# Row-wise infinity norm: the last 128 rows as a block of their own, transposed on VectorE and stored as one line

## The chip, the core and the metric

The kernel runs on one core of a Trainium2 chip. The metric is the device time of one execution in microseconds (us); the time of a kernel is the median over its runs. Profiles are of one execution each. PE is TensorE, DVE is VectorE, ACT is ScalarE, POOL is GpSimd, SP is SyncE.

## The reference

```python
def setup_inputs():
    return {"x": np.random.randn(8192, 8192).astype(np.float32)}

def reference(x):
    return np.linalg.norm(x, ord=np.inf, axis=1)
```

With a vector per row, this is the largest absolute value of each of the 8192 rows: 256 MiB (268.4 MB) in, 32 KB out.

## The kernel before

The work is one stream. SyncE issues loads of x into a ring in SBUF (`ring`, three places of 16384 columns, 128 partitions), and VectorE reduces each landed load with an absolute maximum (`Pieces.reduce`, line 110 in the profile). `Pieces.load` (line 92) issues the loads. There are five semaphores for loads, `SEMS = 5`, each counting one load at a time: load i is issued once the reduction of load i - 5 is done, and once the reductions that still read its place in the ring are done. The first three loads wait for nothing.

The rows come in two groups. The first 46 x 128 = 5888 rows are the big ones: partition p holds 46 rows that follow each other in memory, and a load brings two of them (`R = 2`, 16384 columns) to each partition, 23 loads in all, reduced by one instruction each into `res_big`. The last 18 x 128 rows are the tail: partition p holds 18 rows that follow each other (`x_tail`), and the loads cut this run of 18 x 8192 columns wherever `tail_loads` puts a cut. `tail_loads` plans the cuts from the end backwards. It has a price for a load (1.1775 ns a column and 0.073 us) and for a reduction (1.0417 ns a column and 0.060 us), and picks each width so that VectorE is done with what came before when the load lands. The planned tail has 29 loads from 16384 columns down to 704, so there are 52 loads in all, 24 of them of 16384 columns.

A load that crosses from one row to the next is reduced by one instruction for each row. A row with several pieces leaves partial results in a tile `parts`, and GpSimd combines them (line 207) into the row's column of `res_tail`. The very last row of each partition is done otherwise: its partial results go to columns of `ring` just behind the place where its last load lands, so that the last reduction takes the 704 landed columns and the 6 partial results in one go, 710 elements, and no combining comes after it.

At the end three stores go out, all of them 128 pieces, one for each partition:

- `early` (line 220, ACT's queue): the 46 columns of `res_big`, 23 KB.
- `middle` (line 224, ACT's queue): the first 16 columns of `res_tail`, 8 KB. It waits for GpSimd's work on these rows.
- `last` (line 239, SyncE's queue): the last two columns of `res_tail`, 1 KB, that is 8 bytes for each partition. It waits for VectorE's last reduction, behind which stand two tiny idle memsets (line 218), and a no-op on line 235 has waited for GpSimd.

`early` and `middle` also wait for the reduction of the third load from the end.

Of the kernel before, what the change touches and what calls it, by code (L numbers as in the profile page):

```python
# [7 lines left out]
P = 128  # L8
R = 2
RING = 3 * 16384  # L10
APART = 2048
SEMS = 5


LOAD = (1.1775e-3, 0.073)
REDUCE = (1.0417e-3, 0.060)
SPARE = 0.08
ROWS = 18
FIRST = 768
SNAP = 0.6  # L20
GRAIN = 64

IDLE = 2


def tail_loads(n_cols, big):

    slack = 0.0
    lag = REDUCE[0] * FIRST + REDUCE[1]
    loads = []
    end = ROWS * n_cols

    def take(top, bottom, most):
        nonlocal slack  # L40
        w = 0
        n = 0
        spare = SPARE if loads else 0
        while True:

            n += 1
            start = max(bottom, (top - 1) // n_cols * n_cols - (n - 1) * n_cols)
            fit = int((lag + slack - spare - REDUCE[1] * n) / REDUCE[0])
            w = max(w, min(fit, top - start) // GRAIN * GRAIN)
            if fit <= top - start or start <= bottom:  # L50
                break
        w = max(GRAIN, min(w, most, top - bottom))
        row = (top - w + n_cols - 1) // n_cols * n_cols
        if top - row >= SNAP * w or (w == most and top > row):
            w = top - row
        n = (top - 1) // n_cols - (top - w) // n_cols + 1
        slack += (LOAD[0] - REDUCE[0]) * w + LOAD[1] - REDUCE[1] * n
        loads.append((top - w, w))
        return top - w

    ends = [take(end, end - n_cols, FIRST), take(end - n_cols, end - 2 * n_cols, n_cols)]
    for top, bottom in zip(ends, (end - n_cols, 0)):
        while top > bottom:
            top = take(top, bottom, big)
    return loads[::-1]


class Pieces:
# [57 lines left out]
@with_exitstack  # L126
def kernel(
    ctx: ExitStack,
    tc: tile.TileContext,
    x: bass.AP,  # L130
    out: bass.AP,
):
    nc = tc.nc
    f32 = mybir.dt.float32
    n_rows, n_cols = x.shape

    tail = tail_loads(n_cols, R * n_cols)
    split = n_rows - ROWS * P
    n_big = split // (R * P)

    x_big = x[:split].rearrange("(p t r) m -> t p (r m)", p=P, r=R)
    x_tail = x[split:].rearrange("(p r) m -> p (r m)", p=P)

    single = ctx.enter_context(tc.tile_pool(name="single", bufs=1))
    ring = single.tile([P, RING + APART], f32)
    res_big = single.tile([P, n_big, R], f32)
    res_tail = single.tile([P, ROWS], f32)
    idle = single.tile([1, IDLE], f32)  # L150
    pieces = Pieces(tc, ring)

    for t in range(n_big):
        at = pieces.room(R * n_cols)
        pieces.load(at, R * n_cols, x_big[t])
        buf = ring[:, at : at + R * n_cols]
        pieces.reduce([(res_big[:, t, :], buf.rearrange("p (r m) -> p r m", r=R))])


    parts = []  # L160
    for i, (start, w) in enumerate(tail):
        c = 0
        while c < w:
            row = (start + c) // n_cols
            n = min(w - c, (row + 1) * n_cols - start - c)
            parts.append((row, i, c, n))
            c += n
    of_row = [[q for q in parts if q[0] == row] for row in range(ROWS)]

    spots, behind, dst = {}, {}, {}
    at = RING
    for row, own in enumerate(of_row):
        if row == ROWS - 1:
            spots[own[-1][1]] = at
            at += own[-1][3]
            for q in own[:-1]:
                dst[q] = ring[:, at : at + 1]
                at += 1  # L180
            behind[own[-1]] = len(own) - 1
            dst[own[-1]] = res_tail[:, row : row + 1]
        elif len(own) == 1:
            dst[own[0]] = res_tail[:, row : row + 1]
        else:
            some = single.tile([P, len(own)], f32, name=f"parts{row}")
            for k, q in enumerate(own):
                dst[q] = some[:, k : k + 1]
    assert at <= RING + APART and len(behind) == 1
    for i, (start, w) in enumerate(tail):  # L190
        at = spots[i] if i in spots else pieces.room(w)
        pieces.load(at, w, x_tail[:, start : start + w])
        done = pieces.reduce(
            [
                (dst[q], ring[:, at + q[2] : at + q[2] + q[3] + behind.get(q, 0)])
                for q in parts
                if q[1] == i
            ]
        )
        for row in range(ROWS - 1):  # L200
            if len(of_row[row]) > 1 and of_row[row][-1][1] == i:
                best = dst[of_row[row][0]]
                more = [dst[q] for q in of_row[row][1:]]
                while more:
                    two, more = more[:2], more[2:]
                    to = best if more else res_tail[:, row : row + 1]
                    combined = nc.gpsimd.tensor_scalar(  # L207
                        out=to,
                        in0=best,
                        scalar1=two[0],  # L210
                        scalar2=two[1] if len(two) == 2 else None,
                        op0=mybir.AluOpType.max,
                        **(dict(op1=mybir.AluOpType.max) if len(two) == 2 else {}),
                    )
                    tc.add_to_no_dep_group("combined", combined.ins)
    tc.declare_fence(done.ins, group="loads")
    for i in range(IDLE):
        tc.keep_in_program_order(nc.vector.memset(idle[:, i : i + 1], 0.0))  # L218

    early = nc.scalar.dma_start(  # L220
        out=out[:split].rearrange("(p q) -> p q", p=P), in_=res_big.rearrange("p t r -> p (t r)")
    )
    out_tail = out[split:].rearrange("(p r) -> p r", p=P)
    middle = nc.scalar.dma_start(
        out=out_tail[:, : ROWS - 2], in_=res_tail[:, : ROWS - 2]
    )
    for store in (early, middle):
        tc.add_manual_dep(
            store.ins,
            pieces.last[-3].name,  # L230
            mybir.DependencyInfo(mybir.DependencyClass.Sync, mybir.DependencyReason.DATA),
            reason="not beside the last load",
        )

    seen = nc.sync.keepalive_nop([nc.sync.lower_ap(res_tail[:, ROWS - 2 : ROWS - 1])])
    tc.keep_in_program_order(seen)
    tc.no_tile_sem_insts.add(seen.ins.name)
    tc.add_to_no_dep_group("seen", seen.ins)
    last = nc.sync.dma_start(out=out_tail[:, ROWS - 2 :], in_=res_tail[:, ROWS - 2 :])
    tc.declare_no_dep(last.ins, group="combined", reason="SyncE has waited for GpSimd")  # L240
    tc.declare_fence(last.ins, group="seen")
# [1 line left out]
_INS = ['x']  # L243
_OUTS = [((8192,), 'float32')]
# [25 lines left out]
```

## Time and profile before

| | |
|---|---|
| median of 3 runs | 629.04 us (628.88 to 629.17) |
| span of the profiled execution, first to last instruction | 627.3 us |
| that execution's own time beside its span | not given apart; the median stands 1.74 us above the span |
| VectorE busy | 552.1 us (88%), 62 instructions |
| GpSimd busy | 3.2 us |
| bytes read from HBM | 268.44 MB, 428 GB/s over the span |

How to read it. The span runs from the first to the last instruction that the profile has; launch and completion lie outside. A group's row gives line, engine, operation, output and input, number, busy time in total, mean duration in nanoseconds, and the idle time of the engine ahead of it with what ended it. A timeline row gives start, duration, engine, line, operation and shape; `SPq` and `ACTq` are the queues of an engine that issues DMAs, and their rows tell of the issue and not of the transfer. A row of the DMA issues gives the number of issues, their size, and the time from issue to landing. Rows of 40 digits cut the stretch asked for into 40 equal slices, each digit being the busy share in tenths.

### The profile page before, as it was taken

The numbers are of one execution on the slowest core, as the hardware profiler recorded it, in microseconds if no ns is written. First come the engines' busy times: TensorE is split into PE (matmuls) and PEld (weight loads), VectorE is DVE, ScalarE is ACT, GpSimd is POOL, SyncE is SP. The second block draws the span as 40 slices with busy tenths as digits, with TensorE's granted clock in tenths as the row PEclk, the third lists the DMA queues.
The fourth block names the chain that finished last, engine by engine and source line by source line (L and its number), as shares of the span: only waits on it lengthen the run. The fifth ranks groups of instructions, "written<-read, shape, count | busy, mean of one in ns | idle before, by whom it ended". The sixth has DMA issues, their size and how long they took to land.

```text
span 627.3 us, 175 instructions
## 1 busy us (share of the span) xinstructions
DVE 552.1 (88%) x62; POOL 3.2 (1%) x14
## 2 busy tenths in 40 slices
DVE  0588988889988889888898888988889999999998
POOL 0000000000000000000000000000000000000000
DMA  9999999999999999999999999999999999999997
GB/s 401 405 464 401 468 401 468 401 468 401 468 401 468 401 468 401 468 401 468 401 460 410 456 414 447 422 443 426 435 424 442 411 430 440 430 424 430 425 423 304
DMA packets 7921, 268.48 MB, mean 428 GB/s; under 512 B 1264, under 2 KB 1264, under 8 KB 2416
## 3 DMA queue, kind: packets, MB, share of 16 engines
q1 hardware_dynamic: 7632, 268.44, 99.3%
q10 hardware_dynamic: 288, 0.03, 0.0%
q14 instruction: 1, 0.01, 0.0%
HBM read 268.44 MB, written 0.03 MB: 428 GB/s over the span
## 4 chain that ended last, share of the span: by engine, by line
DMA 57%; DVE 42%; issue 0%; DVEq 0%; SPq 0%
DMA ring<-in_x_dram 57%; DVE res_big L110 22%; DVE parts L110 12%; DVE res_tail L110 7%; DVE ring L110 1%; DVEq L265 0%; SPq L92 0%; DVE idle L218 0%
## 5 line engine op out<-in xcount | busy, mean ns | idle before, releaser
L110 DVE TENSOR_REDUCE res_big<-ring 128x2 f32<-128x16384 f32 x23 | 396.1, 17220 | 69.6 <-DMA ring<-in_x_dram 69.6
L110 DVE TENSOR_REDUCE parts<-ring 128x1 f32<-128x3136 f32 (+18 forms) x22 | 78.5, 3633 | 1.2 <-DMA ring<-in_x_dram 1.2
L110 DVE TENSOR_REDUCE res_tail<-ring 128x1 f32<-128x8192 f32 (+1 forms) x9 | 69.8, 7811 | 2.1 <-DMA ring<-in_x_dram 2.1
L110 DVE TENSOR_REDUCE ring<-ring 128x1 f32<-128x1600 f32 (+5 forms) x6 | 8.3, 1445 | 0.0
L207 POOL TENSOR_SCALAR res_tail<-parts 128x1 f32<-128x1 f32 x9 | 2.7, 296 | 615.7 <-DVE parts L110 615.7
L207 POOL TENSOR_SCALAR parts<-parts 128x1 f32<-128x1 f32 x1 | 0.4, 353 | 5.6 <-DVE parts L110 5.6
L254 POOL MEMSET const-bfloat16-1.0<- 128x1 bf16 x1 | 0.1, 102 | 0.0
L254 POOL MEMSET const-uint8-127<- 128x1 uint8 x1 | 0.1, 101 | 0.0
L254 POOL MEMSET const-float32-0.0<- 128x1 f32 x1 | 0.1, 98 | 0.2 <-issue 0.2
L254 POOL MEMSET const-float32-1.0<- 128x1 f32 x1 | 0.1, 98 | 0.0
L218 DVE MEMSET idle<- 1x1 f32 x2 | 0.1, 59 | 0.0
## 6 DMA issues: line engine op xcount, KB each, us to landing
ring<-in_x_dram SPq DMA_DIRECT2D x3, 4096.0 KB, 40.5
ring<-in_x_dram SPq DMA_DIRECT2D x1, 7264.0 KB, 31.1
ring<-in_x_dram SPq DMA_DIRECT2D x1, 5024.0 KB, 33.3
ring<-in_x_dram SPq DMA_DIRECT2D x1, 4544.0 KB, 34.5
ring<-in_x_dram SPq DMA_DIRECT2D x1, 4224.0 KB, 40.3
ring<-in_x_dram SPq DMA_DIRECT2D x1, 4032.0 KB, 35.5
ring<-in_x_dram SPq DMA_DIRECT2D x1, 3584.0 KB, 35.4
ring<-in_x_dram SPq DMA_DIRECT2D x2, 1568.0 KB, 18.3
```

Source lines behind the costliest of these rows:

```text
L110: ins = self.nc.vector.tensor_reduce(out=dst, in_=src, axis=mybir.AxisListType.X, op=mybir.AluOpType.max, apply_absolute_value=True,)
L207: combined = nc.gpsimd.tensor_scalar(out=to, in0=best, scalar1=two[0], scalar2=two[1] if len(two) == 2 else None, op0=mybir.AluOpType.max, ...
L218: tc.keep_in_program_order(nc.vector.memset(idle[:, i : i + 1], 0.0))
L254: nc = _bacc.Bacc("TRN2", target_bir_lowering=False, num_devices=1)
```

## The change

The tail is divided. The 17 x 128 rows ahead of the last 128 keep the layout with rows that follow each other in a partition (`x_tail`, now 17 rows a partition). The last 128 rows are a block of their own, one row for each partition (`x_last`). So the results of the last block are 128 numbers that lie beside each other in the output. The last reduction writes them to column 0 of a new tile `res_last` (128 x 32, cleared by a memset at the start of the kernel); four VectorE transposes of 32 x 32 bring that column into one partition of a tile `line` (32 x 128), and SyncE stores this partition's 512 bytes in one piece. The transposes stand between the last reduction and the idle memsets.

`tail_loads` is gone, and a written list `TAIL` has the widths: 29 loads, now from 11392 and 15744 down to 704 and 640, with an 832 among them. With 23 big loads there are again 52. The order at the end is changed: the last 704 columns of row 16, the last of the 17, are loaded next to last, after all but the last 640 columns of the last block. Both of these rows now use the columns of `ring` behind their last load for partial results: row 16 has 4 of them, the last block 7. In the built program the tail has 44 reductions where it had 37, and GpSimd has 13 combining operations where it had 10.

`middle` now stores all 17 columns of `res_tail` in pieces of 68 bytes. Its wait for the third load from the end is gone; it waits for the reduction of row 16, which is the next to last, and for GpSimd. The no-op that waited for GpSimd on SyncE is gone, and SyncE's store waits for the last transpose.

```diff
-tail = tail_loads(n_cols, R * n_cols)
-split = n_rows - ROWS * P
+ROWS = 17
+TAIL = [11392, 15744, 14016, 12480, 11136, 9856, 8832, 7872, 6976, 6208, 5440, 4864, 4352, 3840]
+TAIL += [3456, 3008, 2688, 2432, 2112, 1856, 832, 1536, 1344, 1152, 1024, 896, 768, 704, 640]
...
+    split = n_rows - (ROWS + 1) * P
+    split_last = n_rows - P
...
-    x_tail = x[split:].rearrange("(p r) m -> p (r m)", p=P)
+    x_tail = x[split:split_last].rearrange("(p r) m -> p (r m)", p=P)
+    x_last = x[split_last:]
...
+    res_last = single.tile([P, 32], f32)
+    line = single.tile([32, P], f32)
+    nc.vector.memset(res_last, 0.0)
...
+    last_row = ROWS * n_cols
+    tail = []
+    at = 0
+    for w in TAIL[:-2]:
+        tail.append((at, w))
+        at += w
+        if at + TAIL[-2] == last_row:
+            at = last_row
+    tail += [(last_row - TAIL[-2], TAIL[-2]), (at, TAIL[-1])]
...
-        if row == ROWS - 1:
+        if row >= ROWS - 1:
             spots[own[-1][1]] = at
...
-            dst[own[-1]] = res_tail[:, row : row + 1]
+            dst[own[-1]] = res_last[:, 0:1] if row == ROWS else res_tail[:, row : row + 1]
...
-        pieces.load(at, w, x_tail[:, start : start + w])
+        of_last = start - last_row
+        src = x_tail[:, start : start + w] if of_last < 0 else x_last[:, of_last : of_last + w]
+        pieces.load(at, w, src)
...
     tc.declare_fence(done.ins, group="loads")
+    for q in range(P // 32):
+        own = slice(q * 32, q * 32 + 32)
+        tc.keep_in_program_order(nc.vector.transpose(out=line[:, own], in_=res_last[own, :]))
     for i in range(IDLE):
         tc.keep_in_program_order(nc.vector.memset(idle[:, i : i + 1], 0.0))
...
-    out_tail = out[split:].rearrange("(p r) -> p r", p=P)
     middle = nc.scalar.dma_start(
-        out=out_tail[:, : ROWS - 2], in_=res_tail[:, : ROWS - 2]
+        out=out[split:split_last].rearrange("(p r) -> p r", p=P), in_=res_tail
     )
-    for store in (early, middle):
-        tc.add_manual_dep(
-            store.ins,
...
+    tc.add_manual_dep(
+        early.ins,
...
-    seen = nc.sync.keepalive_nop([nc.sync.lower_ap(res_tail[:, ROWS - 2 : ROWS - 1])])
...
-    last = nc.sync.dma_start(out=out_tail[:, ROWS - 2 :], in_=res_tail[:, ROWS - 2 :])
-    tc.declare_no_dep(last.ins, group="combined", reason="SyncE has waited for GpSimd")
-    tc.declare_fence(last.ins, group="seen")
+    nc.sync.dma_start(out=out[split_last:].rearrange("(o q) -> o q", o=1), in_=line[0:1, :])
```

## The prediction

> **What bounds the kernel now.** I began with the page: which engine is busy, then the slices and the chain.
>
> ```profile
> span 627.3 us, 175 instructions
> DVE 552.1 (88%) x62; POOL 3.2 (1%) x14
> DMA  9999999999999999999999999999999999999997
> ...
> HBM read 268.44 MB, written 0.03 MB: 428 GB/s over the span
> ```
>
> The DMA row is full in 39 slices of 40: the input stream sets the length, and VectorE (DVE), 88% busy, follows it. The chain that ended last gives the pace.
>
> ```profile
> 59.27 40.78 DMA ring<-in_x_dram
> 100.06 0.03 issue
> 100.08 17.23 DVE res_big L110
> ...
> 623.38 0.71 issue
> 624.09 0.89 DVEq L265
> 624.97 0.01 DVE idle L218 x2
> ```
>
> Its pieces start again every 58.05 us, which is three loads of 16384 columns: 19.35 us a load, 1.18 ns a column. VectorE takes 17.23 us for the same columns. It needs 0.89 of a load's time, so a load that follows one of w columns may be as short as some 0.89 w before VectorE falls behind. Small loads cost something beyond their bytes on both sides. The rest is the end of the span, by the timeline and the DMA issues of its last microseconds.
>
> ```profile
> 623.35 0.38 ACTq L220 DMA_DIRECT2D out_dram<-res_big  x1
> 623.77 0.45 ACTq L224 DMA_DIRECT2D out_dram<-res_tail  x1
> 624.09 0.88 DVE L110 TENSOR_REDUCE res_tail<-ring 128x1 f32<-128x710 f32 x1
> 624.35 0.36 POOL L207 TENSOR_SCALAR res_tail<-parts 128x1 f32<-128x1 f32 x1 [10.82 <-DVE parts L110]
> 624.92 0.06 DVE L218 MEMSET idle<- 1x1 f32 x2
> 625.00 0.35 SPq L239 DMA_DIRECT2D out_dram<-res_tail  x1
> ```
>
> ```profile
> ring<-in_x_dram SPq DMA_DIRECT2D x1, 352.0 KB, 4.1
> out_dram<-res_big ACTq DMA_DIRECT2D x1, 23.0 KB, 1.7
> out_dram<-res_tail ACTq DMA_DIRECT2D x1, 8.0 KB, 2.4
> out_dram<-res_tail SPq DMA_DIRECT2D x1, 1.0 KB, 1.5
> ```
>
> The last load (704 columns, 352 KB) was issued at 619.97 and landed 4.1 us later, at 624.07. Its reduction starts at 624.09 and ends at 624.97, the last store is issued at 625.00 and lands 1.47 us later (1.5 in the row) at 626.47, and the span ends at 627.3, 0.8 us behind. So 3.2 us of the span lie behind the stream. The change can move the time in two places only: the 624 us of stream, and these 3.2 us. The median of the runs, 629.04, stands 1.74 us above the span of 627.3; I make the sum on the span and add 1.74.
>
> **The stream.** Bytes and number of loads stay: 24 + 28 = 52 before, 23 + 29 = 52 after, each with one row of each of 128 partitions, so whatever a load costs beyond its bytes is paid 52 times in both. What could lengthen the stream is a queue that runs dry, since a load is issued when the reduction five loads back, and what lay in its part of the ring, are done. I stepped through the new list with the prices of the rows. A reduction of 256 columns takes 409 ns and one of 768 takes 942, so 1.041 ns a column and 142 ns fixed, of which 83 overlap the one before (624.09 lies 0.08 before 623.23 + 0.94): 0.06 us each. A load: the 24th had landed at 467.75, where its reduction starts in the timeline, and the last at 624.07, so 28 loads brought 131072 columns in 156.3 us; with 19.35 us for 16384, that makes 1.176 ns a column and 0.076 us a load. The same stepping puts the last reduction of the kernel before at 624.06, where the timeline has 624.09. With the new list it gives: VectorE idle only once in the tail (3.0 us before the load of 15744); from there every reduction within 0.1 us of its landing, but for the 832 columns, 1.0 us late and caught up at the next load; each of the last loads issued at least 2.8 us before the one ahead of it lands (before: 3.2). The first load took about 1 us from issue to its first bytes, so the queue does not run dry. The tail has 44 reductions instead of 37; 7 x 0.06 = 0.4 us, within VectorE's idle time. The last load lands at 624.05: **0.0**.
>
> New is the address pattern of the last 8192 columns: rows 32 KB apart, where the tail before has 18 rows (576 KB) and the big loads 46 rows (1.5 MB) between partitions. The trace shows the same rate at both of those, as the stepping with a single price fits both. The Trainium skill (DMA: Bandwidth & Descriptors, Latency and other measured facts) speaks against powers of two: 207 instead of 214 GB/s at a pitch of 512 KiB, 103 at 4 MiB. Its nearest case, 3.3% on the last block, would add an estimated 0.3 us; no run here shows such a pitch. By the rows, the last block costs 8192 x 1.18 = 9.7 us, 0.1 us for each per cent that it slows. From above, the slices of the page go down to 401 GB/s where the mean is 428, 6.3% or +0.6 us; from below 0, since no row shows the stream faster than its pace. I take 0, by the two pitches that the trace has.
>
> **Behind the last landing, on the path.** *Last reduction*: 640 columns and 7 partial results instead of 704 and 6, so 647 instead of 710 elements: 63 x 1.041 ns = **-0.06 us**, end at 624.91.
>
> *Four transposes*, 32x32 each, between the reduction and the store. The first waits for the reduction's own completion, 0.02 us by the chain's "issue" pieces. The trace has no transpose. From below: four idle memsets at 59 ns, 0.24 us. From above: four of GpSimd's one-column operations at 296 ns, 1.18 us. The nearest row is VectorE's own reduction: 142 ns fixed + 32 x 1.041 = 175 ns alone, 92 with the overlap, so 175 + 3 x 92 = 0.45 us. A transpose must take in its block before it gives it out, which argues for more; I take **+0.50** and the wait's **+0.02**, and the last transpose ends at 625.43. The memsets now run behind it and SyncE doesn't wait for them (**-0.01**).
>
> The Trainium skill (VectorE: DVE Perf Modes, The TRN2 errata) gives about 150 cycles fixed at 0.96 GHz. That would be an estimated (150 + 32) / 0.96 = 190 ns each with nothing overlapped, 0.76 us for the four; the overlap of 0.08 us in the rows above speaks for less.
>
> *Store*, one line of 512 bytes instead of 128 pieces of 8 bytes. The DMA view of 625.00 to 626.60 shows where the 1.47 us went (a digit is 0.04 us):
>
> ```profile
> DMA  0000000000000000000003543100000000000000
> ...
> q1 hardware_dynamic: 144, 0.00, 4.8%
> ```
>
> Packets run from 625.84 to 626.04: 0.84 us of making descriptors, 0.20 of packets, 0.43 of confirmation. One packet takes away nearly all of the 0.20, and with one share instead of 16 there is no last of 16 to wait for: **-0.22**, landing 1.25 after the issue. From below I allow 1.0 (descriptors made faster too), from above the 2.4 of the 8 KB store.
>
> *Other stores.* `middle` now carries row 16 of the tail and waits for the reduction before the last: 623.23 + 0.88 = 624.11 instead of 623.77. With its 2.4 us it lands at 626.55, 0.15 before the line store; it is the next late one, and would take over if the line landed sooner. ACT has nothing queued behind it. SyncE's wait for GpSimd goes; it ended when the operation of 624.35 was done, 0.27 before VectorE, so nothing comes of it. GpSimd's 3 more operations of 0.3 us and the memset of `res_last`, which runs in the 22.7 us that VectorE waits for its first load, are hidden.
>
> **Sum.** -0.06 + 0.02 + 0.50 - 0.01 - 0.22 = +0.23 us: issue at 625.45, landing at 626.70, span 627.5, time 629.04 + 0.23 = 629.3. Ends of the unknown terms: transposes at 0.24 and a landing in 1.0 give -0.3 us, or 628.7; transposes at 1.18 alone give +0.9, or 629.9, and the slower last block with them +1.5, or 630.5; a landing in 2.4 alone gives +1.4, or 630.4.
>
> **Rivals.** What this kernel's measurement can tell from no change is about 0.2%, 1.26 us.
> 1. *The line store lands late.* It goes through one share of one queue, and whatever delays that share delays the end. For it: the 8 KB store took 2.4 us and the 23 KB store before it 1.7, so size does not decide. Against: the 1 KB store, alone in time, took 1.5. At 2.4 us the sum is +1.4 us, 630.4; with transposes at 0.45 it crosses 1.26 from a landing of 2.35 us. Slower.
> 2. *The stream slows in the tail*, by the new pitch or by loads issued too late. From 13% on the last block (1.26 / 9.7) it crosses the bound; half of that gives 629.9. Against: the full DMA row at two pitches, and 2.8 us of cover. At 13%, 630.5. Slower.
> 3. *The end shrinks.* A store that lands in 1.0 us and transposes at 0.24 give 628.7, but then `middle` holds the end at 626.55, and the time is 629.1. To gain 1.26 of the 3.2 us behind the stream would need the store nearly free. Only a faster stream, which the single price per column does not suggest, gives 627.7.
>
> **How the numbers follow.** The sum above, within 0.2%: 0.64. Rival 1: 0.17, and rival 2: 0.14, of which a part stays within the bound; together they give slower 0.26 and same 0.05. Rival 3: 0.05, nearly all of it faster by a cause I don't see (0.04). So faster 0.04, same 0.70, slower 0.26. The time is that of the sum, 629.3; the range goes from 628.7 (both end terms low) to 630.5 (one rival in full).
>
> **What would show it.** In the changed profile: last reduction starting at 624.1 and ending at 624.9; four transposes within 0.5 us; a store of 0.5 KB with 1.2 to 1.3 us to landing; VectorE waiting for DMA once, some 3 us, in the tail; span 627.5. A last reduction starting later than 624.3 makes the stream's step wrong; transposes over 0.2 us each, or a landing over 1.5, the end's.

## The result and the profile after

The changed kernel takes 630.15 us (630.02 to 630.5, 14 runs) against 628.9 us (628.78 to 629.17, 14 runs) in the same session: a ratio of 1.002, 95% interval 1.0013 to 1.0027. That is 1.25 us more, just at the 0.2% that I had set for "no change", and inside the range. The interval leaves out 1, so the loss is real, if small. The forecast time, 629.3, was 0.85 us too low.

The first lines of the page of the changed kernel, to be held against those of the kernel before:

```profile
span 628.4 us, 191 instructions
DVE 553.5 (88%) x74; POOL 4.0 (1%) x17
DMA  9999999999999999999999999999999999999997
HBM read 268.44 MB, written 0.03 MB: 427 GB/s over the span
```

The span is 1.1 us longer, the DMA row as full as before. Its timeline from 624.5 us on (start, duration, engine, line, operation):

```profile
623.91 0.88 DVE L64 TENSOR_REDUCE res_tail<-ring 128x1 f32<-128x708 f32 x1
624.71 0.82 DVE L64 TENSOR_REDUCE res_last<-ring 128x1 f32<-128x647 f32 x1
624.89 0.34 ACTq L197 DMA_DIRECT2D out_dram<-res_tail  x1
625.56 0.84 DVE L190 STREAM_TRANSPOSE line<-res_last 32x32 f32<-32x32 f32 x4
626.36 0.07 DVE L192 MEMSET idle<- 1x1 f32 x2
626.43 0.32 SPq L206 DMA_DIRECT2D out_dram<-line  x1
```

Three things are to be read off. The last reduction starts at 624.71 and not at 624.09, so 0.62 us were lost ahead of it, in the stream. Four transposes take 0.84 us. And the store is issued at 626.43; SyncE's waits tell when it landed (engine, line, what it waited for: total, times, longest):

```profile
SPq L230 <- DMA out_dram<-line: 0.7, 1, 0.7
```

SyncE's issue ends at 626.75, the next instruction is through at 626.83, and 0.7 us later the store has landed: 627.54, 1.11 us after the issue, where the 8-byte pieces took 1.47.

| from the two traces | before | after | step |
|---|---|---|---|
| last reduction starts | 624.09 | 624.71 | +0.62 |
| last reduction takes | 0.88 | 0.82 | -0.06 |
| from its end to the store's issue | 0.03 | 0.90 | +0.87 |
| from issue to landing | 1.47 | 1.11 | -0.36 |
| span | 627.29 | 628.36 | +1.07 |

The remaining 0.18 us of the 1.25 belong to the one profiled run of the kernel before. In all runs on record with both numbers the time stands 1.73 to 1.83 us above the span, so its span of 627.29 goes with a time of about 629.07, which is 0.17 above the median of 628.9.

Where the 0.62 us come from, the waits show (window from 500 us to the end, the changed kernel first, then the kernel before):

```profile
DVE parts L64 <- DMA ring<-in_x_dram: 0.7, 1, 0.7
```

```profile
DVE parts L110 <- DMA ring<-in_x_dram: 1.2, 1, 1.2
```

The wait of the kernel before ended at 496.8, ahead of a reduction that reaches into the window; from there to the end its VectorE waits for no load. The wait of the changed kernel lies inside the window, and the timeline of VectorE from 570 to 585 us puts it in its place:

```profile
579.26 5.88 DVE L64 TENSOR_REDUCE parts<-ring 128x1 f32<-128x1984 f32 x2 [0.72 <-DMA ring<-in_x_dram]
```

This is the load of 5440 columns, a width with nothing special, well ahead of the last block. It landed 7.34 us behind the one before it, where 5440 x 1.176 ns + 0.076 = 6.47. In the DMA view of 576 to 577 us a second queue appears:

```profile
q1 hardware_dynamic: 21, 0.46, 110.9%
q14 instruction: 1, 0.01, 2.0%
```

The kernel before has it in its last three microseconds and nowhere else in its span (view of 624.3 to 625.3 us):

```profile
q14 instruction: 1, 0.01, 1.9%
```

In the changed kernel it is one packet of 8 KB of instructions, 576.17 to 576.50. The row packets of that load took 0.81 to 0.82 us each on their share of the queue, except one, which started at 576.49 and took 1.47. Each load has 16 completions. Ahead of the packet the last of them follows the one before it by 0.05 us; from this load on by 0.86 to 0.91, and still so three loads from the end. The share that had met the packet did not catch up, and a load counts as landed when its last share is there. In the last two loads the distance falls to 0.40 and 0.10 us, because the other shares come later there; the loads themselves still land at their price, 0.87 and 0.80 us apart where it gives 0.90 and 0.83. This became theory B; its rivals were the widths, the row pitch, and the code of another engine.

### The profile page after: what moved, and what is told of

It reads as the page before. It is cut to its first block, busy times and chain, and to the rows that moved or that the text cites. A ratio compares the mean times of both kernels' runs of the same rounds, so it can differ in the third digit from the quotient of the medians.

```text
span 628.4 us, 191 instructions
## 1 busy us (share of the span) xinstructions
DVE 553.5 (88%) x74; POOL 4.0 (1%) x17
## 4 chain that ended last, share of the span: by engine, by line
DMA 59%; DVE 40%; issue 0%; DVEq 0%
DMA ring<-in_x_dram 59%; DVE res_big L64 22%; DVE parts L64 11%; DVE res_tail L64 4%; DVE ring L64 3%; DVE res_last L64 0%; DVE line L190 0%; DVEq L230 0%; DVE idle L192 0%
## 5 line engine op out<-in xcount | busy, mean ns | idle before, releaser
L64 DVE TENSOR_REDUCE parts<-ring 128x1 f32<-128x3712 f32 (+23 forms) x27 | 104.6, 3938 | 3.6 <-DMA ring<-in_x_dram 3.6
L64 DVE TENSOR_REDUCE res_tail<-ring 128x1 f32<-128x8192 f32 (+1 forms) x5 | 35.6, 7117 | 0.0
L64 DVE TENSOR_REDUCE ring<-ring 128x1 f32<-128x1088 f32 (+10 forms) x11 | 16.4, 1566 | 0.0
```

Source lines behind the costliest of these rows:

```text
L64: ins = self.nc.vector.tensor_reduce(out=dst, in_=src, axis=mybir.AxisListType.X, op=mybir.AluOpType.max, apply_absolute_value=True,)
```

## The experiments

Spans are of one profiled execution, ratios of the medians against the kernel before in the same session. The place of the instruction packet (one packet of 8 KB in the span, in every profile) and the last reduction's start are what tells the theories apart:

| run | VectorE instructions in the program (the profile lists 2 fewer in each) | packet at, us | last reduction starts | span |
|---|---|---|---|---|
| before | 71 | 624.87 | 624.09 | 627.29 |
| changed | 84 | 576.17 | 624.71 | 628.36 |
| e1 no transposes, 128 pieces | 80 | 576.02 | 624.58 | 633.32 |
| e2 changed + 24 on VectorE | 108 | 394.20 | 624.54 | 628.19 |
| e3 before + 24 on VectorE | 95 | 413.74 | 624.75 | 627.90 |
| e4 changed + 24 on GpSimd | 84 | 576.20 | 624.75 | 628.40 |
| e5 changed, one transpose | 81 | 576.23 | 624.78 | 628.30 |
| e6 own block, old cuts, four transposes | 76 | 624.43 | 624.02 | 627.75 |
| e7 the same, one transpose | 73 | 624.48 | 624.07 | 627.66 |
| e8 before, 4-byte pieces | 71 | 624.57 | 624.12 | 627.27 |
| e9 e6 + 8 on VectorE | 84 | 550.60 | 624.67 | 628.39 |
| e10 new widths, shorter code | 76 | 582.71 | 624.83 | 628.36 |
| e11 before + 24 on GpSimd | 71 | 624.55 | 624.05 | 627.20 |
| e12 new widths, shorter still | 74 | 582.58 | 624.68 | 628.20 |

**e1.** The end without the transposes.

```diff
-    for q in range(P // 32):
-        own = slice(q * 32, q * 32 + 32)
-        tc.keep_in_program_order(nc.vector.transpose(out=line[:, own], in_=res_last[own, :]))
...
-    nc.sync.dma_start(out=out[split_last:].rearrange("(o q) -> o q", o=1), in_=line[0:1, :])
+    nc.sync.dma_start(out=out[split_last:].rearrange("(p o) -> p o", o=1), in_=res_last[:, 0:1])
```

> The changed kernel without the four transposes: the 128 results of the last block go out in 128 pieces of 4 bytes, straight from the column that the last reduction writes. Theory A (the end of the span is a chain of a wait, four transposes of 0.20 us one behind the other, and a store): the store is issued 0.87 us sooner after the last reduction and lands in about 1.47 us as the 8-byte pieces of the kernel before did, instead of 1.11; the span shrinks from 628.4 by 0.87 - 0.36 = 0.5 us to 627.9. Rival (the one-line store is not quicker by itself, the store lands in 1.1 us here too): 627.5. In both the last load still lands near 624.6, since nothing of the stream is touched, if the 0.56 us there do not hang on the transposes.

Measured: 635.28 us, ratio 1.0101 (1.0084 to 1.0118), span 633.3. Both expected spans, 627.9 and 627.5, were more than 5 us too low. The issue came as early as expected, 0.03 us after the last reduction (0.90 with the transposes). The landing did not; the row of the issue in the timeline, and the last row of the DMA issues (KB, us to landing):

```profile
625.42 0.35 SPq L203 DMA_DIRECT2D out_dram<-res_last  x1
```

```profile
out_dram<-res_last SPq DMA_DIRECT2D x1, 0.5 KB, 7.1
```

So 128 pieces of 4 bytes side by side in the output land in 7.1 us. With the results of a block beside each other, leaving the transposes out is no alternative; e8 asks why.

**e2, e3, e4.** Whose code is in the packet? The same 24 one-element memsets ahead of everything, on VectorE in the changed kernel (e2) and in the kernel before (e3), on GpSimd in the changed one (e4).

```diff
+    pad = single.tile([1, 24], f32)
+    for i in range(24):
+        tc.keep_in_program_order(nc.vector.memset(pad[:, i : i + 1], 0.0))    # e4: nc.gpsimd
     pieces = Pieces(tc, ring)
```

> The changed kernel with 24 one-element memsets on VectorE ahead of everything, in the 22 us in which it waits for its first load. Theory B (the 8 KB instruction packet at 576.2 us, which holds up one share of the load stream by 0.86 us, is VectorE's own code, fetched when it reaches a fixed place in it): the packet comes about 24 instructions sooner, near 400 to 450 us, in the big loads; the stream still ends late, span 628.3 to 628.6. Rival C (it is the code of another engine, or comes by time): the packet stays at 576 us. The memsets by themselves cost nothing.

> The kernel before with the same 24 memsets on VectorE ahead of everything. Theory B: the instruction packet, which came at 624.87 us, behind the stream, moves 24 VectorE instructions up, to about 550 to 590 us, where it holds up one share of the stream: the last load lands 0.5 to 0.9 us later and the span goes from 627.3 to about 628.0. Rival C (not VectorE's code): the packet stays behind the stream and the span stays at 627.3. Rival D (the packet does not hold up the stream at all, and the late landing of the changed kernel has to do with its widths or its row pitch): the packet moves and the span stays at 627.3.

> The changed kernel with 24 one-element memsets on GpSimd ahead of everything. Theory B (VectorE's code): the instruction packet stays at 576 us, span 628.4. Rival C (GpSimd's code): the packet comes sooner, when GpSimd starts its combining at about 500 us or ahead of it, and the span stays at 628.3 to 628.6 as long as the packet falls into the stream.

Measured, each in one run: e2 span 628.2, packet at 394 us. e3 span 627.9 and 629.68 us, packet at 414 us. e4 span 628.4, packet at 576 us, unmoved. So it is VectorE's code. And e3 is the causal half: nothing but memsets that run while VectorE waits for its first load, and the end of the kernel before shifts (timeline of e3):

```profile
624.75 0.88 DVE L110 TENSOR_REDUCE res_tail<-ring 128x1 f32<-128x710 f32 x1
625.58 0.06 DVE L221 MEMSET idle<- 1x1 f32 x2
625.66 0.35 SPq L242 DMA_DIRECT2D out_dram<-res_tail  x1
```

The last reduction starts 0.66 us later than before, and the span grows by 0.61. In e2 the packet falls into the big loads, where VectorE has 2 us of idle time a load, and still the last reduction starts 0.45 us later than in the kernel before: the loss is the share's and not VectorE's. Details of the expectations were off: in e2 I had put the packet at 400 to 450 us and the span at 628.3 or more, and in e3 I had put the packet at 550 to 590 us, counting 24 instructions back from its old place. It came at 414, where VectorE has started 47 instructions; in e2 and in the changed kernel it is 47 as well, in the kernel before 64.

**e5.** One transpose of the whole tile.

```diff
-    line = single.tile([32, P], f32)
+    line = single.tile([P, 32], f32)
...
-    for q in range(P // 32):
-        own = slice(q * 32, q * 32 + 32)
-        tc.keep_in_program_order(nc.vector.transpose(out=line[:, own], in_=res_last[own, :]))
+    tc.keep_in_program_order(nc.vector.transpose(out=line, in_=res_last))
...
-    nc.sync.dma_start(out=out[split_last:].rearrange("(o q) -> o q", o=1), in_=line[0:1, :])
+    nc.sync.dma_start(out=out[split_last:].rearrange("(o q) -> o q", q=32), in_=line[0:P:32, :])
```

> The changed kernel with one transpose of the whole 128 x 32 tile instead of four of 32 x 32 (it leaves each block's row in a partition of its own, 0, 32, 64 and 96), and a store of four lines of 128 bytes. Theory A (each transpose takes 0.20 us whatever its partitions, and they do not overlap): the store is issued 0.63 us sooner after the last reduction; with a landing in 1.1 us the span goes from 628.4 to 627.8, the time from 630.15 to 629.5. Rival E (the cost of a transpose grows with its blocks, or four lines land as late as 128 pieces): 628.4 or more. The stream is left as it is: instruction packet at 576 us, last load near 624.5.

Measured: 630.05 us, ratio 1.0018 (1.0009 to 1.0027), span 628.3. From its timeline and SyncE's waits:

```profile
625.63 0.21 DVE L188 STREAM_TRANSPOSE line<-res_last 128x32 f32<-128x32 f32 x1
625.87 0.62 SPq L204 DMA_DIRECT2D out_dram<-line  x1
```

```profile
SPq L228 <- DMA out_dram<-line: 0.9, 1, 0.9
```

The transposes were right: one of 128 x 32 costs what one of 32 x 32 does, 0.21 us, and the store is issued 0.27 us behind the last reduction instead of 0.90. The store took it back: the issue of four lines holds SyncE's queue for 0.62 us, where one line took 0.32 and 128 pieces 0.35, and the landing comes 1.60 us after the issue (625.87 to 627.47) instead of 1.11. So four lines do land late, as rival E had it for this half. The time goes ahead of the data: the first packet of the four lines starts 1.22 us after the issue, that of the one line 0.75. Why four lines take longer to issue than 128 pieces is not settled.

**e6, e7.** The block of its own on the cuts of the kernel before, with four transposes and one line, and with one transpose and four lines.

```diff
     tail = tail_loads(n_cols, R * n_cols)
...
-            dst[own[-1]] = res_tail[:, row : row + 1]
+            dst[own[-1]] = res_last[:, 0:1]
...
+        of_last = start - last_row
+        src = x_tail[:, start : start + w] if of_last < 0 else x_last[:, of_last : of_last + w]
...
```

The transposes and the stores are those of the changed kernel (of e5 in e7), only that `middle` still waits for the reduction of the third load from the end.

> The block of its own, the four transposes and the one-line store, on the cuts that the kernel before plans (18 rows, 29 loads, ending with 768 and 704): the change without its other widths. VectorE has 7 reductions fewer than in the changed kernel. Theory B with the packet coming at a fixed place in VectorE's code whenever the code is longer than in the kernel before: the packet falls into the stream and the last load lands 0.5 us late, span 628.4 to 628.5 (last reduction 0.07 us longer than in the changed kernel). Theory B2 (the packet comes late, as in the kernel before, as long as the code is only 5 instructions longer): last load at 624.05, span 627.29 + 0.87 - 0.01 - 0.36 = 627.8, time 629.4. Rival D (the late landing comes from the row pitch of the last block or of the 17 rows): the last load is late without an instruction packet in the stream.

> The same with one transpose of 128 x 32 and a store of four lines of 128 bytes. By theories A and B2: wait and transpose 0.23 us, landing 1.1 instead of 1.47, so span 627.29 + 0.23 - 0.36 = 627.15, time 628.8, by 0.1 us below the kernel before. By theories A and B: 627.7 to 627.8, time 629.4.

Measured: e6 629.53 us, ratio 1.0009 (0.9999 to 1.0018), span 627.7, the number of theory B2; e7 629.41 us, ratio 1.0007 (0.9998 to 1.0015), span 627.7, where 627.15 was expected, because its four lines land late again (625.23 to 626.83). In both the packet comes behind the stream and the last reduction starts on time, so the first form of theory B, a fixed place in VectorE's code whenever that is longer than before, does not hold. The timeline of e6:

```profile
624.02 0.88 DVE L110 TENSOR_REDUCE res_last<-ring 128x1 f32<-128x710 f32 x1
624.28 0.36 POOL L215 TENSOR_SCALAR res_tail<-parts 128x1 f32<-128x1 f32 x1 [10.80 <-DVE parts L110]
624.67 0.34 ACTq L234 DMA_DIRECT2D out_dram<-res_tail  x1
624.94 0.84 DVE L227 STREAM_TRANSPOSE line<-res_last 32x32 f32<-32x32 f32 x4
625.73 0.07 DVE L229 MEMSET idle<- 1x1 f32 x2
625.80 0.32 SPq L245 DMA_DIRECT2D out_dram<-line  x1
```

This separates the two halves of the change. Own block, transposes and line cost 0.46 us of span; the other 0.6 come with the rest. It also settles the row pitch: rows 32 KB apart in the last block and 17 rows a partition in the tail are both here, and the stream ends as early as before.

**e8.** The kernel before, its last store with one column instead of two.

```diff
-        out=out_tail[:, : ROWS - 2], in_=res_tail[:, : ROWS - 2]
+        out=out_tail[:, : ROWS - 1], in_=res_tail[:, : ROWS - 1]
...
-    last = nc.sync.dma_start(out=out_tail[:, ROWS - 2 :], in_=res_tail[:, ROWS - 2 :])
+    last = nc.sync.dma_start(out=out_tail[:, ROWS - 1 :], in_=res_tail[:, ROWS - 1 :])
```

> The kernel before, with only its last column in the last store: 128 pieces of 4 bytes, 72 bytes apart, and 17 columns in the store ahead of it. It tells why the store of 128 pieces of 4 bytes beside each other took 7.07 us to land. Theory F (pieces beside each other write into the same short stretch of memory and wait for each other): 72 bytes apart they land in about 1.5 us, span 627.3. Theory G (4 bytes are slow as such, being less than 8): they land in about 7 us again, span 633.

Measured: span 627.3, 629.05 us in one run. The row of the DMA issues:

```profile
out_dram<-res_tail SPq DMA_DIRECT2D x1, 0.5 KB, 1.4
```

The same number of 4-byte pieces, 72 bytes apart, lands in 1.4 us. So the size of a piece is not what costs 7.1 us; that the pieces lie side by side is the difference that I see, though the two stores also read from different tiles, in different kernels. The traces put the delay behind the packets: the last packet of e1 is done at 626.47, 1.05 us after the issue, and the 16 completions come between 628.51 and 632.49; in e8 the packets are done 1.05 us after the issue as well, and all completions within another 0.37 us. That the pieces wait for each other in the memory is my reading.

**e9.** The decisive pair with e6: the same cuts, block and transposes, plus 8 memsets on VectorE at the start.

```diff
+    pad = single.tile([1, 8], f32)
+    for i in range(8):
+        tc.keep_in_program_order(nc.vector.memset(pad[:, i : i + 1], 0.0))
```

> The block of its own with four transposes on the cuts of the kernel before, as in the run with span 627.7, plus 8 one-element memsets on VectorE ahead of everything, which bring VectorE's code from 76 to the changed kernel's 84 instructions. Theory B (the length of VectorE's code decides whether its next 8 KB are fetched in the middle of the stream or behind it): the packet leaves 624.4 us and falls into the stream, at the 46th instruction or so, between 545 and 570 us; the last load lands 0.5 to 0.7 us later, span 628.3, time 630.1, as the changed kernel has, though the widths are those of the kernel before. Rival D (the widths of the changed kernel cost the 0.6 us): span 627.7, time 629.5.

Measured: 630.17 us, ratio 1.0019 (1.0009 to 1.0029), span 628.4; e6 had 629.53. From the DMA view of 550.4 to 551.4 us and the timeline of the end:

```profile
q14 instruction: 1, 0.01, 2.0%
```

```profile
624.67 0.88 DVE L110 TENSOR_REDUCE res_last<-ring 128x1 f32<-128x710 f32 x1
625.58 0.84 DVE L230 STREAM_TRANSPOSE line<-res_last 32x32 f32<-32x32 f32 x4
626.45 0.32 SPq L248 DMA_DIRECT2D out_dram<-line  x1
```

Eight hidden memsets bring 0.65 us, the whole distance between e6 and the changed kernel, without any of its widths. No run of e9 (630.03 to 630.34) comes near one of e6 (629.34 to 629.61). The packet went from 624.4 to 550.6 us.

**e10, e11, e12.** What decides where the packet falls? e10 and e12 take VectorE instructions out of the changed kernel (boundaries of loads moved onto rows, one transpose, the clearing memset on GpSimd, no idle memsets; e12 also combines row 16 on GpSimd). e11 adds 24 memsets on GpSimd to the kernel before.

```diff
-TAIL = [... 14016, 12480, ... 4864, 4352, 3840] + [3456, ...]
+TAIL = [... 14016, 12480, ... 4736, 4480, 3712] + [3584, ...]     # e10
+TAIL = [... 13824, 12672, ... 4736, 4480, 3712] + [3584, ...]     # e12
...
+        tc.keep_in_program_order(nc.gpsimd.memset(pad[:, i : i + 1], 0.0))    # e11, 24 times
```

> The changed kernel with its widths (29 loads; four of them moved by 128 columns so that two rows have a piece less), one transpose of 128 x 32 with a store of four lines, no idle memsets, and the clearing memset on GpSimd: VectorE's code has 76 instructions instead of 84. To be compared with the run with one transpose and 81 instructions, whose span was 628.3 with the packet at 576 us. Theory B: the packet comes behind the stream, near 624.5 us, the last reduction starts at 624.1 to 624.2 instead of 624.78, and the span is 627.7, the time 629.5. Rival D (the widths as such): last reduction at 624.8 and span 628.3 still.

> The kernel before with 24 one-element memsets on GpSimd ahead of everything; VectorE's code stays at 71 instructions. The packet has come at one of two places in VectorE's order, with 46 to 48 of its instructions started or with 64, and the run with the changed widths and 76 VectorE instructions showed the first although a kernel with 76 had shown the second: so the length of VectorE's code alone does not decide. Theory B3 (the length of the whole program decides, all engines taken together: 184 to 188 instructions with the late place, 191 and more with the early one; here 208): the packet moves from 624.9 to about 598 us, VectorE's 47th instruction, the last load lands 0.5 to 0.7 us later, span 627.9, time 629.7. Theory B4 (something in VectorE's own code decides): the packet stays behind the stream, span 627.3, time 629.0.

> The widths of the changed kernel once more (six of them moved by 128 or 192 columns, so that three rows have a piece less), the block of its own with one transpose and four lines, row 16 combined on GpSimd as in the kernel before, no idle memsets: 74 instructions on VectorE, and ACT without its second wait. If the packet now comes behind the stream (near 624.5 us, with 64 of VectorE's instructions started), theory B expects the last reduction at 624.1 to 624.2 and a span of 627.7, as with the cuts of the kernel before; rival D (the widths cost the 0.6 us by themselves) expects 624.8 and 628.3 though the packet is late. If the packet stays in the stream, near 583 us, both expect 628.3, and what decides its place stays open.

Measured: e10 630.14 us (ratio 1.0017, 1.0007 to 1.0026), e12 630.09 us (1.0019, 1.001 to 1.0029), e11 628.92 us (0.9999, 0.999 to 1.0009). In e10 and e12 the packet stayed in the stream, although VectorE's code is no longer than in e6, and so e10 missed the span of 627.7 that theory B had expected; in e11 it stayed behind it, so the length of the whole program does not decide (theory B3 falls). What stays open is the rule. In the fourteen profiles the packet comes with 46 to 48 of VectorE's instructions started, or with 64. All kernels with 60 reductions and at most 5 VectorE instructions more than the kernel before show the second, all others the first; length alone does not explain e10 and e12. For the same reason the new widths could not be run without a packet in the stream: that they cost nothing by themselves is argued, from the 0.62 us being all there in e9, and not shown. One sign is left of a cost that the late share may hide: in e9 the last but one completion of the last load comes at 623.83, as in e6, and in the changed kernel at 624.51.

## Why the prediction was right, and where it was not

It held in its verdict and its range, but by a sum whose terms missed in both directions, and in part by luck: the loss that decided came by a way that no rival had, and it ended 0.01 us short of the 1.26 that I had set for "no change".

- **The stream, "0.0".** This step failed. Its own mark, a last reduction later than 624.3, was met with 624.71. Bytes, the 52 loads, the price of each and the pace of VectorE were as stated: e6 ends its stream on time with the new address patterns, and the one load off its price in the changed kernel is the one that met the packet. The last load was issued 2.8 us before the one ahead of it landed, as stated; why the other shares still came later in the last two loads is open. What I left out was VectorE's own code as a load on the same 16 queues. I had counted "7 reductions more" only as 0.4 us of VectorE's time. The trace of before did show the packet, one of 8 KB at 624.87 in the last microseconds, and I passed over it.
- **Four transposes, +0.50 and the wait's +0.02.** Wait and transposes measured 0.87. The wait was right at 0.03. A transpose alone takes 200 ns where I had 175, and the size was off because I gave them the overlap of 0.08 us that reductions have; they start 0.21 apart. The Trainium skill's fixed cost (VectorE: DVE Perf Modes, The TRN2 errata), which I had weighed as 0.76 us and set aside, was the better price: an estimated 190 ns against 200 here, and nothing overlapped.
- **The store, -0.22.** Direction right, size low: -0.36, landing in 1.11. The store is one data packet and one completion, two packets on SyncE's queue, instead of 144. The 0.20 of packets fell to 0.03, and what I had left as it was shrank too: 0.75 us ahead of the first packet for 0.84, and 0.33 behind the last for 0.43. The Trainium skill (DMA: Bandwidth & Descriptors, Why a DMA increments its semaphore by 16 and not by 1) says that a DMA runs on the largest number of DMA engines, at most 16, that divides the slowest dimension of both of its sides, and that only the full count of 16 means that all data has landed. The two packets agree with one engine.
- **`middle`.** Predicted to land 0.15 us ahead of the line store; it landed at 626.33, 1.2 ahead. Its 2.4 us in the kernel before were no property of the store: in e3, which has the same store and its packet elsewhere, it takes 1.5. In the kernel before 15 of its 16 completions are in by 625.31 and the last comes at 626.21. That the packet at 624.87 held up this one share is my reading of that.
- **Rivals.** Rival 1, a line store of 2.4 us, rested on that same row and falls with it. Rival 2 named the right place, the stream in the tail, with the wrong causes: e6 has the new pitch without the loss, and e9 the loss with the old widths and the other 15 shares on time. Rival 3 did not come.

With the terms as measured, 0.62 - 0.06 + 0.87 - 0.36 = 1.07 us, the sum closes on the span. Without the stream's 0.62 it is 0.45, where I had +0.23, and e6 measured 0.46. The forecast time is only 0.85 us off, and not 1.02 as the step is (1.25 for 0.23), because its base of 629.04, from three runs, stands 0.14 above the median of 14.

## What to carry to other kernels

Where a stream of loads keeps every queue full, a code fetch of 8 KB in the middle of it costs the end of the kernel some 0.6 us (e3, e9), so look for the instruction queue in the DMA view by windows, and read "a few more instructions, all hidden" as a change in when it comes. Before a result is brought into a neat line for its store, price the way there: 0.87 us of wait and transposes bought 0.36 us of landing. Of the two stores of 128 pieces of 4 bytes seen here, the one with its pieces side by side in the output is the form to avoid (7.1 us), and the one with them apart is not (1.4).

## What the runs showed of the hardware that I had not expected

- One instruction packet of 8 KB, 0.33 us long, puts one of the 16 shares of the stream behind, and it stays behind: its completion comes 0.7 to 0.8 us behind the others in e3 and e9 until near the end (0.1 in e6), and the last reduction 0.66 and 0.65 us later. The Trainium skill (Runtime: NRT & Kernel Launch, Instruction fetch mechanics) calls the cost of crossing into an engine's next block of code mostly hidden. For the engine that holds here: no wait of VectorE is put down to its code. For the stream of loads it does not hold.
- 128 pieces of 4 bytes landed in 7.1 us side by side (e1) and in 1.4 us when 72 bytes apart (e8).
- A transpose of 128 x 32 takes 0.21 us, as much as one of 32 x 32 (0.20), and four in a row started 0.21 us apart, without overlap (e5, changed).
- The issue of a store of four lines from four partitions held SyncE for 0.62 us, one line 0.32, 128 pieces 0.35 (e5, changed, e1).
